# Block 2 of a two-block transformer: where x's norm and transposes stand, and a pool for the merged features

## The chip, the cores and the metric

The kernel runs on one core of a Trainium2 chip. Its time is that of one execution on the device, in microseconds (us). The core's engines are TensorE (PE; its weight loads are shown as PEld), VectorE (DVE), ScalarE (ACT), GpSimd (POOL) and SyncE (SP), whose queue issues the DMAs.

## What is computed

Block 1 (two layers on 256 tokens of x) is not touched. Block 2 works on x and on 256 tokens of a context, ctx, in two layers; only x is returned, so layer 1 doesn't update ctx.

```python
for l in range(2):
    with_ctx = l < 1
    # sh, sc, g: shift, scale, gate of x; csh, csc, cg: of ctx
    u, uc = x * (1 + sc1) + sh1, ctx * (1 + csc1) + csh1
    y, yc = token_mixer(u, uc, ...)   # conv, mLSTM, attention branches; gated merge; @ w_out + b_out
    x = layer_norm(alpha * x + g1 * y, ln1_g, ln1_b)
    x = layer_norm(alpha * x + g2 * sq_relu_mlp(x * (1 + sc2) + sh2, w1, b1, w2, b2), ln2_g, ln2_b)
    if with_ctx:
        ctx = layer_norm(alpha * ctx + cg1 * yc, ln1_g, ln1_b)
        ctx = layer_norm(alpha * ctx + cg2 * sq_relu_mlp(ctx * (1 + csc2) + csh2, ...), ln2_g, ln2_b)
```

The width is 1024, the feed-forward's 4096. All is float32; a product is made of three matmuls on high and low halves.

## The kernel before

**Tokens.** Block 2 holds four tiles of 128 tokens, `self.res[0..3]`: 0 and 1 are ctx, 2 and 3 are x. In transposed tiles (features on partitions) ctx has columns 0 to 255 and x columns 256 to 511. Layer 0 works on all four, layer 1 needs ctx only as a source of keys, values and states, so its later parts work on x's 256 columns alone.

**Products.** `w` loads a weight tile of 512 KB (`wr`, SP's queue), ScalarE makes its high half (`wh`, L323), and VectorE the low half (`wl`, L326); while the counter `self.spare` is positive, GpSimd makes `wl` instead. Four buffers of each rotate. `mm3` (L331 to L333) issues the three matmuls. `tiles` (L350) works several weight tiles over column ranges that are given as `parts`.

**From tokens to u.** `ln` (L955 to L972) makes a token tile's norm: statistics on VectorE, the power -0.5 on GpSimd (L368), the two halves of the row on ScalarE (L970) and VectorE (L972). `make_u` (L933 to L940) takes a stream (two token tiles) in four steps; a step has four transposes on PE into a PSUM tile `tp` (two of them exist), a scale and shift by ScalarE (L938) and VectorE (L940), and the split into high (`uh`, ScalarE, L391) and low (`ul`, VectorE, L392). `uT` takes `uh` and `ul` from a pool that holds one pair of 512 columns.

**The order in a layer.** `layer` runs: make_u of what is left; `residual` (GpSimd, L885 to L902); `mixer2`, which merges three gated branches into `macc` (L1019, L1020) and splits it (L1474 and on) into a pair from `uT`; then w_out (`for n in range(2)`), whose products `tail` (L1562 to L1565) adds to the tokens. For n = 0 one group of matmuls serves all tokens, for n = 1 each token is a group, in the order 3, 2, 1, 0, with its norm behind it. Then a pool `ff` opens, u is made again, and `mlp` runs: `up` and `down` over eight chunks of 512 hidden features. The first chunk's four tiles are worked for x's columns first, then for ctx's. The last `down` of layer 0 has two groups of 48 matmuls, tokens 0 and 1, then 2 and 3. When `mlp` is over the four tokens are normed, and layer 1 starts with make_u of ctx, then of x; its mixer begins with two tiles of `w_in`, for ctx's columns and then for x's.

**What sets the order.** A planner orders each engine's instructions ahead of the run. It goes by the place in the program, an instruction that stands earlier going first, and by its own estimate of when an instruction is ready; one that is estimated to be ready may pass one that isn't. On the chip every engine works its list in order. Pools of tiles are stacked: a pool that opens where another was closed gets its space, and waits for its last reader. `mixer2`'s last pool of gates (`sh`, tiles `sg`) is closed right before the pool `tl` of w_out opens at its place.

## Time and profile before

| | us |
|---|---|
| median of three runs | 2396.82 (2395.77 to 2398.0) |
| the profiled execution | 2396.18 |
| its span, first to last instruction | 2394.4 |
| PE busy | 2310.1 |
| DVE busy | 1747.2 |
| ACT busy | 1195.4 |
| POOL busy | 382.0 |

The profile is that of one execution. A row of its timeline gives the start in us from the span's start, the length, the engine, the line, the operation, what it writes and reads, and in brackets how long the engine stood still before it and what it waited for. Matmuls overlap, so a matmul's length is not its cost; the distance of two starts is. PEclk is the granted clock of TensorE as a share of 2.4 GHz; it is 1.00 or, at the lower level of 1.2 GHz, 0.50, and a window's value is the mean.

### The profile page before, as it was taken

Reading aid. Unit: us, or ns where it says so; the run is one execution under the profiler, and the core shown is the slowest. Engines: PE = TensorE matmul, PEld = TensorE weight load, DVE = VectorE, ACT = ScalarE, POOL = GpSimd, SP = SyncE. Lnnn points to the kernel's source line nnn. Section 1 sums busy time; section 2 is a strip of 40 time slices with the busy share of each in tenths; the row PEclk is TensorE's granted clock in tenths of the full one; section 3 lists DMA queues with packets and bytes.
Section 4 is the critical chain, followed back from the end, with each engine's and each line's share of the span. In section 5 each row is a group of like instructions: output and inputs, shape, how many; then the busy total and the mean of one; then the engine's idle time right before and its main releaser. Section 6 shows DMA issues by size and latency. Waiting matters only on the chain. (4 is left out here: it accounts for less than half of the span.)

```text
span 2394.4 us, 35555 instructions
## 1 busy us (share of the span) xinstructions
PE 2310.1 (96%) x13796; PEld 1965.8 (82%) x13796; DVE 1747.2 (73%) x2632; ACT 1195.4 (50%) x1827; POOL 382.0 (16%) x230
## 2 busy tenths in 40 slices
PE   7999999999999999999999998999998999998997
PEld 6899978888999888788777876777787888897896
DVE  7876778897666589946745559777658996857657
ACT  6766667774465544443443324333334455645553
POOL 4522324550000110000000035000005000003102
PEclk9999999999999999999999999999999999999999
DMA  7544546775555553222214434565433433446553
GB/s 260 180 158 153 161 161 207 248 245 185 185 177 186 188 175 106 75 80 72 87 46 145 136 117 137 181 199 175 127 96 115 150 103 115 133 150 195 188 189 106
DMA packets 120665, 364.64 MB, mean 152 GB/s; under 512 B 28529, under 2 KB 30321, under 8 KB 120497
## 3 DMA queue, kind: packets, MB, share of 16 engines
q1 hardware_dynamic: 120496, 362.38, 47.4%
q8 instruction: 108, 1.77, 0.3%
q14 instruction: 61, 0.49, 0.1%
HBM read 359.05 MB, written 3.28 MB: 151 GB/s over the span
## 5 line engine op out<-in xcount | busy, mean ns | idle before, releaser
L323 ACT CAST wh<-wr 128x1024 fp32r<-128x1024 f32 (+1 forms) x544 | 566.4, 1043 | 791.7 <-PE mm L332 424.0
L326 DVE TENSOR_TENSOR wl<-wr,wh 128x1024 fp32r<-128x1024 f32 x528 | 677.3, 1287 | 325.2 <-ACT wh L323 320.1
L332 PE MATMUL mm<-ul,wh 128*128 128x256 f32 (+1 forms) x2224 | 709.4, 321 | 6.4 <-DVE ul L392 6.4
L333 PE MATMUL mm<-uh,wl 128*128 128x256 f32 (+1 forms) x2224 | 707.9, 320 | 2.6 <-DVE wl L326 2.6
L331 PE MATMUL mm<-uh,wh 128*128 128x256 f32 (+1 forms) x2224 | 704.6, 323 | 4.8 <-ACT uh L424 2.2
L332 PEld LDWEIGHTS mm<-ul,wh 128*128 128x128 f32 x2224 | 421.0, 189 | 45.6 <-DVE ul L392 7.5
L331 PEld LDWEIGHTS mm<-uh,wh 128*128 128x128 f32 x2224 | 415.8, 190 | 47.7 <-issue 7.1
L333 PEld LDWEIGHTS mm<-uh,wl 128*128 128x128 f32 x2224 | 420.2, 189 | 40.6 <-issue 5.2
L332 PE MATMUL mm<-wl,hh 128*128 128x512 f32 x640 | 252.9, 395 | 2.8 <-DVE wl L326 2.8
L331 PE MATMUL mm<-wh,hh 128*128 128x512 f32 x640 | 253.4, 397 | 0.0
L333 PE MATMUL mm<-wh,hl 128*128 128x512 f32 x640 | 253.2, 396 | 0.0
L847 POOL TENSOR_TENSOR macd<-macd,mpr 128x512 f32<-128x512 f32 x108 | 181.6, 1682 | 202.2 <-ACT mpr L846 115.2
L332 PE MATMUL mm<-wl,uh 128*128 128x256 f32 (+1 forms) x672 | 203.5, 304 | 5.8 <-DVE wl L326 5.8
L331 PE MATMUL mm<-wh,uh 128*128 128x256 f32 (+1 forms) x672 | 203.9, 306 | 2.2 <-ACT qk L541 1.5
L843 DVE SCALAR_TENSOR_TENSOR macd<-mr,silu_c,macd 128x512 f32<-128x512 f32 x228 | 189.3, 867 | 22.3 <-POOL macd L847 10.7
L333 PE MATMUL mm<-wh,ul 128*128 128x256 f32 (+1 forms) x672 | 200.8, 301 | 0.1
L331 PEld LDWEIGHTS mm<-wh,hh 128*128 128x128 f32 x640 | 120.8, 189 | 35.1 <-issue 7.5
L332 PEld LDWEIGHTS mm<-wl,hh 128*128 128x128 f32 x640 | 120.8, 189 | 31.7 <-DVE wl L326 3.1
L333 PEld LDWEIGHTS mm<-wh,hl 128*128 128x128 f32 x640 | 120.7, 189 | 28.8 <-issue 0.8
L332 PEld LDWEIGHTS mm<-wl,uh 128*128 128x128 f32 x672 | 127.8, 190 | 14.7 <-DVE wl L326 7.8
L1062 DVE SCALAR_TENSOR_TENSOR cy<-hpad,vecl,cy 128x512 f32<-128x512 f32 (+1 forms) x240 | 138.0, 609 | 0.1
L331 PEld LDWEIGHTS mm<-wh,uh 128*128 128x128 f32 x672 | 127.3, 190 | 12.7 <-ACT qk L541 2.8
(295 smaller groups left out, 3053.6 us busy)
## 6 DMA issues: line engine op xcount, KB each, us to landing
wr<-in_m SPq DMA_DIRECT2D x128, 512.0 KB
wr<-in_w SPq DMA_DIRECT2D x128, 512.0 KB
wr<-in_w_in SPq DMA_DIRECT2D x116, 512.0 KB
mr<-in_w_mod SPq DMA_DIRECT2D x96, 512.0 KB
wr<-in_a_wqkv SPq DMA_DIRECT2D x72, 512.0 KB
wr<-in_b_win SPq DMA_DIRECT2D x24, 512.0 KB
wr<-in_w_out SPq DMA_DIRECT2D x16, 512.0 KB
wr<-in_w_uq SPq DMA_DIRECT2D x16, 384.0 KB
```

The source lines that it names most:

```text
L323: nc.scalar.copy(hi[:, :n], raw[:, :n])
L326: e.tensor_tensor(lo[:, :n], raw[:, :n], hi[:, :n].bitcast(F32), ALU.subtract)
L331: mm(out, lh, rh, start=first, stop=False)
L332: mm(out, lh, rl, start=False, stop=False)
L333: mm(out, ll, rh, start=False, stop=last)
L843: nc.vector.scalar_tensor_tensor(out=a, in0=raw[:, k], scalar=sc, in1=a, op0=ALU.mult, op1=ALU.add)
L847: nc.gpsimd.tensor_tensor(a, a, pr, ALU.add)
L1062: nc.vector.scalar_tensor_tensor(out=ys[ft], in0=src, scalar=wk, in1=ys[ft], op0=ALU.mult, op1=ALU.add)
```

## The change

Four things change in block 2. (1) In layer 0's last `down` the group of tokens 2 and 3 comes first; behind its tails `ready` starts layer 1 (vector load, affine), norms tokens 2 and 3 and makes x's u, and behind the second group it does the same for ctx. The norm and make_u at the start of layer 1 go. (2) Layer 1's first `tiles` has four tiles (two more of the conv branch), x's columns of all four first, then ctx's columns of the first two. (3) The merged features get tiles `mo_h` and `mo_l` in the pool `tl`, split when the mixer is over; u for the feed-forward is taken ahead of w_out, and make_u of x stands right behind token 2's norm, that of ctx behind token 0's. (4) In that pool the gate rows have two buffers, not six.

```diff
@@ -350,8 +350,10 @@
     def tiles(self, aps, uh, ul, c0, c1, parts):
 
         Ws, pts = [], []
-        for k0, k1, a, b in parts:
+        for k0, k1, a, b, *of in parts:
             for i, ap in enumerate(aps):
+                if of and i not in of[0]:
+                    continue
                 if len(Ws) == i:
                     Ws.append(self.w(ap, KT, P))
                     pts.append(self.ps())
@@ -682,7 +684,7 @@
         o, n = self.vat[name]
         return self.vs[:, o:o + n]
 
-    def mlp(self, uh, ul, c0, c1, w1, w2, bias, evac, first):
+    def mlp(self, uh, ul, c0, c1, w1, w2, bias, evac, first, ready=None):
 
         nc, n = self.nc, c1 - c0
 
@@ -713,7 +715,7 @@
         def down(hc, hid):
             groups = [([nn], range(n // P)) for nn in range(2)]
             if hc == 7 and bias is not None:
-                groups = [([0, 1], range(j, j + 2)) for j in range(0, n // P, 2)] if n == 512 else [([0, 1], [j]) for j in range(2)]
+                groups = [([0, 1], [j, j + 1]) for j in (2, 0)] if n == 512 else [([0, 1], [j]) for j in range(2)]
             if hc == 7 and n == 256 and bias is not None:
                 self.spare = TE
             Ws = {}
@@ -728,6 +730,8 @@
                 for nn in nns:
                     for j in js:
                         evac(j, nn, hc, pts[nn, j])
+                if hc == 7 and n == 512:
+                    ready(js)
                 if hc == 7 and nns == [0]:
                     self.halfway()
                 self.tick(MT)
@@ -865,13 +869,13 @@
         self.gdr[l] = self.t(self.dp, [2, 6, D], f"gdr{l}")
 
 
-    def row(self, ap):
-        r = self.t(self.lp, [P, D], "row", bufs=6)
+    def row(self, ap, bufs=6):
+        r = self.t(self.lp, [P, D], "row", bufs=bufs)
         self.nc.sync.dma_start(r, ap.broadcast_to([P, D]))
         return r
 
-    def gate_row(self, l, sub, s):
-        return self.row(self.gdr[l][1 - s:2 - s, sub * 3 + 2, :])
+    def gate_row(self, l, sub, s, bufs=6):
+        return self.row(self.gdr[l][1 - s:2 - s, sub * 3 + 2, :], bufs)
 
     def residual(self, l, sub, toks, prev):
 
@@ -1401,8 +1405,12 @@
                 nc.sync.dma_start(self.tabq, A["c_tab"][:, 0:512])
                 nc.sync.dma_start(tabk, A["c_tab"][:, 512:1536])
                 self.spare = SP[2]
-                tis = [0, 1] + ([T_CONV, T_CONV + 1] if l == 0 else [])
-                p1, p2, *pre = self.tiles([A[f"w_in_{l}"][ti, 0] for ti in tis], uh, ul, 0, 512, ((0, KT, 0, 256), (0, KT, 256, 512)))
+                tis = [0, 1, T_CONV, T_CONV + 1]
+                p1, p2, *pre = self.tiles([A[f"w_in_{l}"][ti, 0] for ti in tis], uh, ul, 0, 512,
+                                           ((0, KT, 0, 256), (0, KT, 256, 512)) if l == 0 else
+                                           ((0, KT, 256, 512), (0, KT, 0, 256, (0, 1))))
+                if l:
+                    pre = [p_[:, 256:512] for p_ in pre]
                 krt = self.t(xg, [P, 512], "krt")
                 h_ = slice(64, 128)
                 for dst, src, ti in ((kr2, p1, 0), (krt, p2, 1)):
@@ -1462,19 +1470,19 @@
             for ft in range(4):
                 self.split(b[0][:, ft, :], b[1][:, ft, :], cy[:, ft, :])
             self.run(self.branch_merge(l, 0, "w_conv", b[0], b[1], acc, uh, ul, sgs))
-        mh, ml = self.uT()
-        for k in range(KT):
-            self.split(mh[:, k, q0:512], ml[:, k, q0:512], acc[:, k, :])
-        return mh, ml
+        return acc
 
     def start(self, l):
 
         self.vl = self.t(self.xp, [P, max(self.A[f"vec{j}"].shape[1] for j in range(2))], "vecl", bufs=2)
         self.nc.sync.dma_start(self.vl[:, 0:self.A[f"vec{l}"].shape[1]], self.A[f"vec{l}"])
         aff = self.affine(l, 0, *((None, None) if l == 0 else (self.vecl(f"prev_g_{l}", 0, KT), self.vecl(f"prev_b_{l}", 0, KT))))
-        self.u = self.uT()
-        yield from self.make_u([0], aff, *self.u)
-        self.aff = aff
+        self.u, self.aff = self.uT(), aff
+
+    def start_ctx(self):
+
+        self.start(0)
+        yield from self.make_u([0], self.aff, *self.u)
         yield
 
     def layer(self, l):
@@ -1484,10 +1492,9 @@
         toks = [0, 1, 2, 3] if l == 0 else [2, 3]
         prev = None if l == 0 else (l - 1) * 6 + 4
         spill = l == 0
-        if l:
-            self.run(self.start(l))
         uh, ul = self.u
-        self.run(self.make_u([1], self.aff, uh, ul))
+        if l == 0:
+            self.run(self.make_u([1], self.aff, uh, ul))
         with tc.tile_pool(name=f"prep{l}", bufs=1) as self.lp:
             self.residual(l, 0, toks, prev)
             if spill:
@@ -1498,14 +1505,19 @@
             self.rc.close()
             self.rp.close()
         with tc.tile_pool(name=f"mix{l}", bufs=1) as self.xq:
-            mh, ml = self.mixer2(l, uh, ul, toks)
+            acc = self.mixer2(l, uh, ul, toks)
             if spill:
                 rp = self.rp.enter_context(tc.tile_pool(name="res1", bufs=1, side="right"))
                 self.res = [self.t(rp, [P, D], f"resb{j}") for j in range(4)]
                 for j in toks:
                     nc.sync.dma_start(self.res[j], xbd[j])
             with tc.tile_pool(name=f"tl{l}", bufs=1) as self.lp:
-                G = {s: self.gate_row(l, 0, s) for s in sorted({j // 2 for j in toks})}
+                mh, ml = (self.t(self.lp, [P, KT, 512 - q0], t, F32R) for t in ("mo_h", "mo_l"))
+                for k in range(KT):
+                    self.split(mh[:, k, :], ml[:, k, :], acc[:, k, :])
+                u = self.uT()
+                aff = self.affine(l, 1, self.vecl(f"ln1_g_{l}", 0, KT), self.vecl(f"ln1_b_{l}", 0, KT))
+                G = {s: self.gate_row(l, 0, s, 2) for s in sorted({j // 2 for j in toks})}
                 for n in range(2):
                     Ws = {}
                     for js in ([toks[::-1]] if n == 0 else [[j] for j in toks[::-1]]):
@@ -1514,17 +1526,17 @@
                             if kc not in Ws:
                                 Ws[kc] = self.w(A[f"w_out_{l}"][n, kc], 2, 512)
                             for j in js:
-                                self.lin_t(pts[j], Ws[kc], 0, 512, mh, ml, j * P, k0=kc * 2, first=kc == 0, last=kc == 3)
+                                self.lin_t(pts[j], Ws[kc], 0, 512, mh, ml, j * P - q0, k0=kc * 2, first=kc == 0, last=kc == 3)
                         for j in js:
                             self.tail(j, n, pts[j], G[j // 2], 0.5)
                             if n == 1:
                                 self.ln([j])
+                                if j % 2 == 0:
+                                    self.run(self.make_u([j // 2], aff, *u))
         with ExitStack() as cx:
             self.xm = cx.enter_context(tc.tile_pool(name=f"ff{l}", bufs=1))
             self.lp = self.xm
-            uh, ul = self.uT()
-            aff = self.affine(l, 1, self.vecl(f"ln1_g_{l}", 0, KT), self.vecl(f"ln1_b_{l}", 0, KT))
-            self.run(self.make_u([1, 0] if l == 0 else [1], aff, uh, ul))
+            uh, ul = u
             with self.behind():
                 G = self.residual(l, 1, toks, l * 6 + 1)
             accs = [self.t(self.xm, [P, D], f"facc{j}") for j in toks]
@@ -1546,13 +1558,20 @@
                 for i in range(2):
                     nc.sync.dma_start(self.last[i], A["rows"][10 + i:11 + i].broadcast_to([P, D]))
             self.spare = SP[1][l]
+
+            def ready(js):
+
+                if l == 0:
+                    if js[0] == 2:
+                        self.drain_bg()
+                        self.start(1)
+                    self.ln(js)
+                    self.run(self.make_u([js[0] // 2], self.aff, *self.u))
             self.mlp(uh, ul, q0, 512, A[f"w1_{l}"], A[f"w2_{l}"], lambda f: self.vecl(f"b1_{l}", f), evac,
-                     ((0, KT, 256, 512), (0, KT, 0, 256)) if l == 0 else ((0, KT, 256, 512),))
+                     ((0, KT, 256, 512), (0, KT, 0, 256)) if l == 0 else ((0, KT, 256, 512),), ready)
             self.drain_bg()
             if l:
                 self.finish()
-        if l == 0:
-            self.ln(toks)
 
     def tail(self, j, n, src, G, f=None):
         e = self.nc.vector
@@ -1621,7 +1640,7 @@
                     self.mixer_b()
                     for j in range(2):
                         self.tap("b1c", self.res[2 + j], j)
-                    self.bg.append(self.start(0))
+                    self.bg.append(self.start_ctx())
                     self.mlp1(1, u2)
                     for j in range(2):
                         self.tap("b1d", self.res[2 + j], j)
```

## Rows read from the trace of the kernel before

**Rows 1.** Engines on the page: busy us, share, instructions.

```profile
PE 2310.1 (96%) x13796; PEld 1965.8 (82%) x13796; DVE 1747.2 (73%) x2632; ACT 1195.4 (50%) x1827; POOL 382.0 (16%) x230
```

**Rows 2.** Waits in stretch A: engine, line, released by; us, times, longest.

```profile
PE tp L933 <- DVE mt L940: 4.9, 1, 4.9
...
PE mm L332 <- DVE ul L392: 2.2, 2, 1.4
```

**Rows 3.** The same view of stretch B.

```profile
PE mm L332 <- DVE ul L392: 4.2, 3, 2.9
PE tp L933 <- DVE mt L940: 4.1, 1, 4.1
```

**Rows 4.** Sums of A, B, dense: busy (count) PE PEld DVE ACT POOL, PEclk.

```profile
1414.81:1451.18 36.37, 29.23 (x226) 28.45 (x224) 27.93 (x28) 17.22 (x27) 32.29 (x14) 0.91 0.41 145
1816.11:1843.71 27.60, 19.27 (x133) 18.38 (x131) 25.05 (x38) 11.10 (x19) 22.23 (x12) 0.88 0.46 155
1846.00:1866.00 20.00, 20.00 (x171) 20.00 (x170) 18.82 (x24) 17.68 (x24) 2.25 (x1) 1.00 0.58 198
```

**Rows 5.** The same sums, around low clock, and one with full clock.

```profile
1418.55:1425.38 6.83, 4.60 (x22) 4.61 (x23) 6.66 (x11) 3.35 (x6) 4.86 (x3) 0.50 0.55 187
1821.32:1824.73 3.41, 3.41 (x16) 3.41 (x17) 3.41 (x11) 2.67 (x5) 1.52 (x3) 0.50 0.90 219
1838.39:1841.80 3.41, 3.41 (x18) 3.41 (x18) 3.17 (x4) 1.49 (x3) 3.41 (x2) 0.50 0.02 5
2000.00:2006.00 6.00, 4.34 (x38) 4.17 (x37) 5.20 (x9) 3.21 (x6) 0.66 (x1) 1.00 0.46 123
```

**Rows 6.** Timeline of PE: start us, us, line, tiles [idle before, releaser].

```profile
1420.78 1.11 PE L933 MATMUL tp<-cst,resb 128*128 128x128 f32 x4 [4.93 <-DVE mt L940]
...
1888.99 0.48 PE L1192 MATMUL mm<-m_q,m_k 128*128 128x256 f32 x1 [3.39 <-DVE m_k L1164]
...
2003.01 0.35 PE L388 MATMUL mm<-cst,l_a 128*128 128x1 f32 x2 [1.66 <-DVE l_a L1273]
...
2189.96 0.48 PE L933 MATMUL tp<-cst,resb 128*128 128x128 f32 x1 [7.29 <-ACT resb L970]
```

**Rows 7.** Timeline of POOL: casts of weights in A and in B.

```profile
1412.01 2.41 POOL L326 TENSOR_TENSOR wl<-wr,wh 128x1024 fp32r<-128x1024 f32 x1 [4.12 <-ACT wh L323]
...
1809.03 2.41 POOL L326 TENSOR_TENSOR wl<-wr,wh 128x1024 fp32r<-128x1024 f32 x1
1811.88 8.27 POOL L326 TENSOR_TENSOR wl<-wr,wh 128x1024 fp32r<-128x1024 f32 x3 [0.44 <-ACT wh L323]
```

**Rows 8.** Timeline of DVE: a norm, second half in A, B.

```profile
1408.06 0.54 DVE L972 TENSOR_SCALAR resb<-resb,bmv,brs 128x512 f32<-128x512 f32 x1
...
1809.92 1.80 DVE L972 TENSOR_SCALAR resb<-resb,bmv,brs 128x512 f32<-128x512 f32 x1
```

**Rows 9.** Lines of DVE in A, B: count, busy us, mean ns.

```profile
L392 DVE TENSOR_TENSOR ul<-mt,uh 128x512 fp32r<-128x512 f32 x8 | 12.6, 1604 | 0.3 <-ACT uh L391 0.2
...
L392 DVE TENSOR_TENSOR ul<-mt,uh 128x512 fp32r<-128x512 f32 x8 | 10.6, 1329 | 0.4 <-ACT uh L391 0.4
```

**Rows 10.** Timeline of DVE: end of the merge, layers 0, 1.

```profile
1368.93 1.46 DVE L392 TENSOR_TENSOR ul<-macc,uh 128x512 fp32r<-128x512 f32 x2
1370.40 0.69 DVE L1019 SCALAR_TENSOR_TENSOR mt<-sg,mm 128x512 f32<-128x512 f32 x1
...
2161.04 0.41 DVE L1019 SCALAR_TENSOR_TENSOR mt<-sg,mm 128x256 f32<-128x256 f32 x1
```

**Rows 11.** Timeline of PE: last branch matmul, first of w_out.

```profile
1369.96 0.40 PE L333 MATMUL mm<-b_h,wl 128*128 128x512 f32 x1
1370.20 0.39 PE L331 MATMUL mm<-wh,uh 128*128 128x512 f32 x1
```

**Rows 12.** Waits of SP's queue at w_out's start, layer 0.

```profile
SPq L870 <- DVE mt L1019: 3.8, 1, 3.8
```

**Rows 13.** Timeline of ACT: a cast of merged features, layer 0.

```profile
1369.05 0.62 ACT L391 CAST uh<-macc 128x512 fp32r<-128x512 f32 x1 [0.86 <-DVE macc L1020]
```

## The prediction, made before the change was built

> **What bounds the kernel now.** I read the page first: TensorE (PE) is busy 96% of the span [rows 1], so only two things can move the end: time in which PE stands still, and time in which it runs at the lower clock. Next came the waits of PE in the two stretches that the change rearranges, then the window sums of these stretches for the granted clock, and last the timelines of DVE and POOL there. I call the stretches A (layer 0, from w_out's last matmul to the end of the feed-forward's first four tiles, 36.37 us), B (from layer 0's last feed-forward matmul to the end of layer 1's first two tiles, 27.60 us) and C (layer 1's w_out to its feed-forward).
>
> In A PE waits 4.9 us at a transpose for the evacuation of the one before it (L940) and 2.2 us at matmuls for the low half of u (L392), 7.1 us in all [rows 2]. In B it is 4.1 + 4.2 = 8.3 us [rows 3]. Nothing else ends PE's idle time there. The reader should see that all waits are on the chain norm, transpose, scale, split of make_u: no weights, no DMA. The mean granted clock is 0.91 in A and 0.88 in B, against 1.00 in a dense stretch [rows 4]. It is the lower level, 1.2 GHz (0.50), for 6.83 us in A and twice 3.41 us in B, after PE had stood for 4.9, 4.1 and 2.9 us [rows 2, 3, 5]; a wait of 1.66 us left the clock at 1.00 [rows 5, 6]. In A the low stretch begins at 1418.55 while PE still stands until 1420.78 [rows 5, 6], so 1425.38 - 1420.78 = 4.6 us are worked at half speed: 2.3 us lost. In B 6.82 us at half speed lose 3.4 us.
>
> So A loses 7.1 + 2.3 = **9.4 us** and B 8.3 + 3.4 = **11.7 us**. A second count agrees: a matmul of 256 columns takes 20.00 / 170 = 0.118 us in the dense stretch [rows 4]; A holds 192 of them (22.6 us) and 32 transposes at some 0.11 us (3.5 us, the spacing of dense ones), so 10.3 of its 36.37 us are not work. At most 21.1 us are to be had, 0.9% of the time.
>
> **Part 1, B.** In layer 0's last down pass x's tokens (2, 3) come first, then ctx's. The group of ctx's tokens is 48 matmuls of 512 columns, each 0.24 us behind the one before [rows 11], so 11 us, and x's norm, 16 transposes and their splits move beneath it. No matmul or transpose is added; 2 x 24 matmuls of the two conv tiles move forward (5.7 us that PE would do just behind, so they only change places). After that PE has x's columns of four tiles, 4 x 24 x 0.118 = 11.3 us, to cover ctx's norm and transposes. Before, the group that ended first had its norm done on DVE at 1811.72 and the group's matmuls lasted to 1816.1, so some 4.4 us remain for four steps of scale and split. Each step occupies DVE for one L940 (some 0.54 us, as the L972 at 1408.06 of the same kind and size [rows 8]) and one L392 (0.73 us [rows 10]), 5.1 us in all, if nobody is in the way.
>
> Somebody is. POOL subtracts the first four weight tiles' low halves from 1809.03 on, 2.4 to 2.8 us each and to 1820.15 [rows 7], and DVE operations are longer whenever POOL works: the second norm pass (L972) took 1.80 us there and 0.54 us at 1408.06, where POOL stood [rows 8]; L392 averaged 1.60 us in A and 1.33 in B [rows 9] against 0.73 a piece at 1368.93, far from any POOL work [rows 10]. The Trainium skill (SBUF — State Buffer, Who interferes with whom) says that a DVE instruction with two SBUF inputs and a GpSimd instruction that reads SBUF exclude each other, the later one blocking fully; the trace agrees in kind, though its means lie below a whole POOL operation. Were the price a whole POOL operation for each of the moved L392, the slower rival below would come out.
>
> With 0.6 to 0.9 us more for each of four L392 (2.4 to 3.5 us), x's u comes 3 to 5 us late for the matmuls behind it. PE works its queue in order, so this shows either as a stall at a transpose inside the down matmuls or at x's first tile, not both. Ctx's part then meets POOL's residual work (L885 to L902), but under 11.3 us of matmuls; I allow 1 us. Left of B's 11.7: **5 us**. Bounds: 1 us (planned well), 11 us (every L392 stalls PE as now); I stay near the middle, as the means [rows 9] are measured in this very contention. Gain in B: **6.7 us**.
>
> What is queued behind the new waits: DVE's tails of ctx's tokens stand behind the splits and free the accumulators which x's third and fourth tile need; these start 5.7 us after the first, which covers that. SP gets the layer's vector load and no other DMA earlier; POOL gets x's rsqrt among its casts in place of ctx's. The conv tiles' inputs come earlier, and layer 1's gate chain has 5.7 us less of matmuls behind it; it ends in a tight spot already, PE's 3.39 us at m_k [rows 6]. Cost between -3 and +3 us; I take none, because m_k depends on the order on DVE and not on the gates.
>
> **Part 2, A.** Make_u of x goes right behind token 2's norm, so its transposes and splits run under w_out's last two groups (24 matmuls of 512 each, 11 us). Here POOL is free until 1412.01 [rows 7], and x's norm is over at 1408.60 [rows 8]: 3.4 us without contention, then some. The u tiles are free since the mixer is over, which is what the own pool is for. I leave 1.5 us for x's part. Ctx's norm still follows the last matmul. In C the same chain, from the last matmul to the first transpose, takes 7.29 us [rows 6], and four steps of make_u some 6 us more, 13.3 in all. The cover is four tiles of x, 11.3 us. So ctx is late by about 2 us: left **3.5 us** of 9.4 (bounds 1 and 8). Gain in A: **5.9 us**.
>
> **Part 3, the pool of the merged features.** This is the price. Before, the splits of macc went into u's tiles while the last branch's matmuls ran, and w_out began without a gap (at 1370.20, 0.24 us behind the branch's last matmul [rows 11], and as closely in layer 1). The new tiles mo_h, mo_l open where the closed pool of the last gates (sg) lay. A tile at that place already shows what this means: the gate row's DMA, first in the same pool, waited 3.8 us in layer 0 for L1019, the last reader of sg [rows 12], and in layer 1 for the same line. So the first split can only start when the last L1019 ends, 1371.09 in layer 0 [rows 10]. Then one cast of 0.62 us [rows 13] and w_out can start at about 1371.8: **1.6 us** of stall, and DVE's low half (0.73 us, behind a 1.2 us weight subtraction or not) adds 0 to 0.9 us. In layer 1 the last L1019 ends at 2161.45 [rows 10], though without the splits in its way it comes about 0.8 us sooner; a cast of half width takes some 0.4 us, so w_out starts at 2161.1 to 2161.9 and not at 2160.2: 0.9 to 1.7 us. Sum 2.5 to 4.2 us. If a stall lets the clock fall (it did not after 1.66 us, it did after 2.9), 1.7 us come on top in one layer: upper bound 6. I take **3.6 us**, a little above the middle. A lower bound below zero has no reason behind it, since the splits were fully hidden before.
>
> **C** is unchanged: layer 1's w_out ends with token 2 and make_u needs both tokens, so the 7.29 us wait for the norm [rows 6] stays; two small affine operations move away, 0 us.
>
> **The sum.** 6.7 + 5.9 - 3.6 = 9.0 us. The profiled execution took 2396.18 us (span 2394.4 and 1.8 around it); 2396.18 - 9.0 = 2387.2. It lies 0.6 us below the median of 2396.82, so the forecast for a median is **2388**.
>
> **The rivals.**
> (a) The waits only move into the matmuls. The planner sets x's transposes by its own estimate of the norm; if DVE is late at every step, PE stands ahead of ready matmuls. With 8 us left in A and 10 in B and 4.5 for the pool: 21.1 - 18 - 4.5, about 1 us slower, 2398, no change to be measured. For it: POOL's casts lie exactly there in B. Against: in A POOL stands for the first 3.4 us. Also here: the planner puts the transposes behind the matmuls after all, so that the change does not do what it says, with 21.1 us lost again and the pool's 3.6: about 2400 if no more cover comes from four tiles, 2394 with it. Chance 0.2.
> (b) Slower. Each moved L392 waits for a whole POOL operation, 2.8 us in B's mean [rows 7], four times at each place, and the clock falls after each: 2 x (11.2 + 2.3) + 5 for the pool = 32 against 21.1, 2396.8 + 11 = 2408. It decides from about 2.0 us per L392 on, where loss and gain are 4.8 us apart; the total lengths of 1.3 to 1.6 us [rows 9] speak against it. Chance 0.07.
> (c) Everything fits: A and B leave 1 us each, the pool 2.5: 21.1 - 4.5 = 16.6 us, 2380. For it: 11 us of matmuls lie over every moved chain. Against: POOL. Chance 0.1.
> The forecast (some 5 to 14 us gained, 2383 to 2392) has 0.63.
>
> **The numbers.** About 0.2% (4.8 us) is what a measurement of this kernel can tell from no change. Faster than 2392.0: the forecast and (c), 0.73. Within 2392.0 to 2401.6: (a), 0.20. Slower: 0.07. The range runs from (c) at 2380 to 2397, which takes in the pool's upper bound together with a left of 7 and 9 us.
>
> **What the changed profile would show.** The waits of PE on L940 and L392 in A and B fall from 15.4 us to some 6; the granted clock over both windows rises above 0.95. New: PE waits at w_out's first matmuls for the casts of mo_h, some 1.6 us in layer 0 and 1 in layer 1, each right behind the last L1019. C's 7.3 us are as before. I am wrong if PE stalls at transposes inside w_out or the last down pass for more than 4 us each, if w_out's stall passes 3 us, or if the wait at m_k grows by what B saves.

## The result, and the profile after

The changed kernel takes 2421.97 us (median; 2421.33 to 2422.76), the kernel before beside it on the same chip 2396.30: a ratio of 1.0104 (95% interval 1.0091 to 1.0116), 25.7 us slower. The prediction said 2388, range 2380 to 2397, with 0.07 for slower. The profiled execution has a span of 2420.97 us for 2394.39.

The page's engines, after (answers to [rows 1]):

```profile
PE 2317.2 (96%) x13787; PEld 1969.5 (81%) x13796; DVE 1753.8 (72%) x2632; ACT 1194.1 (49%) x1827; POOL 381.6 (16%) x230
```

The work is the same; PE is busy 7 us longer and stands some 20 us longer. PE's waits over the whole span, after (what waited, released by; us, times, longest):

```profile
PE tp L855 <- issue: 13.3, 1, 13.3
PE mm L332 <- DVE wl L326: 8.9, 10, 3.1
PE mm L332 <- DVE ul L394: 7.9, 5, 3.5
PE tp L1150 <- DVE g_li L1142: 7.2, 1, 7.2
PE tp L937 <- ACT resb L974: 7.2, 1, 7.2
PE tp L937 <- DVE mt L944: 7.2, 3, 4.6
```

L855 is the matmul of ones behind layer 1's modulation (L851 before), L1150 the transposes of the gate rows (L1146), L937 make_u's transposes (L933), L394 the low halves (L392). Of the three longest single waits, the prediction has the 7.17 us at L937, takes the place of the 7.19 us for safe, and doesn't name that of the 13.34 us at all. PE's timeline, after, at the gaps (start, length, [idle before, releaser]):

```profile
1370.93 0.47 PE L331 MATMUL mm<-wh,mo_h 128*128 128x512 f32 x1 [1.58 <-ACT mo_h L393]
...
1418.84 1.11 PE L937 MATMUL tp<-cst,resb 128*128 128x128 f32 x8 [2.17 <-DVE mt L944]
1423.92 0.39 PE L332 MATMUL mm<-ul,wh 128*128 128x256 f32 x1 [3.49 <-DVE ul L394]
...
1463.14 1.89 PE L855 MATMUL tp<-macd,cst 128*32 128x512 f32 x2 [13.34 <-issue]
...
1831.66 1.97 PE L937 MATMUL tp<-cst,resb 128*128 128x128 f32 x8 [4.61 <-DVE mt L944]
...
1872.83 0.39 PE L331 MATMUL mm<-uh,wh 128*128 128x256 f32 x1 [2.31 <-ACT g_z L1118]
...
1909.10 0.64 PE L1150 MATMUL tp<-cst,g_li 36*128 36x36 f32 x4 [7.19 <-DVE g_li L1142]
...
2183.83 0.47 PE L331 MATMUL mm<-wh,mo_h 128*128 128x512 f32 x1 [1.42 <-ACT mo_h L393]
...
2213.89 1.97 PE L937 MATMUL tp<-cst,resb 128*128 128x128 f32 x8 [7.17 <-ACT resb L974]
```

Window sums, after: A, the low clock around the 13.34 us, the 27.9 us behind layer 0's last FF matmul (B was 27.6), the low clock at the gate rows (columns as in [rows 4]):

```profile
1416.67:1449.80 33.13, 27.47 (x216) 27.02 (x216) 28.71 (x33) 16.50 (x26) 24.56 (x11) 0.95 0.55 208
1451.84:1468.91 17.07, 5.54 (x9) 2.18 (x9) 17.07 (x7) 1.70 (x2) 16.99 (x7) 0.50 0.19 57
1827.06:1855.00 27.94, 20.75 (x150) 20.34 (x150) 22.73 (x38) 10.61 (x16) 18.57 (x9) 0.88 0.44 142
1905.82:1916.06 10.24, 5.37 (x17) 4.15 (x18) 10.18 (x25) 5.65 (x16) 0.15 (x2) 0.50 0.45 148
```

A itself became 3.2 us shorter (33.13 for 36.37). The loss lies behind it. I cut every trace at the same points: w_out's first and last matmul of layer 0; the tenth of the modulation's twelve matmuls of ones, which stands in the dense middle of FF (the expectation of v2 calls it the sixth); FF's last matmul; the first scores (`m_q,m_k`). "Start of FF" is from w_out's last matmul to that tenth, "border" from FF's last matmul to the first scores.

| us | before | after | difference |
|---|---|---|---|
| to w_out's first matmul | 1370.20 | 1370.93 | 0.7 |
| w_out | 44.77 | 45.73 | 1.0 |
| start of FF | 247.95 | 256.18 | 8.2 |
| rest of FF | 153.35 | 154.21 | 0.9 |
| border | 72.72 | 85.36 | 12.6 |
| the rest | 505.40 | 508.56 | 3.2 |

The first row differs by up to 4 us between kernels that are alike up to there (1366.6 to 1370.7 in those without the new pool), so it proves nothing by itself.

### The profile page after: what moved, and what is told of

Its sections match the earlier page's. It is cut to its first block, busy times and chain, and to the rows that moved or that the text cites. A ratio compares the mean times of both kernels' runs of the same rounds, so it can differ in the third digit from the quotient of the medians.

```text
span 2421.0 us, 35549 instructions
## 1 busy us (share of the span) xinstructions
PE 2317.2 (96%) x13787; PEld 1969.5 (81%) x13796; DVE 1753.8 (72%) x2632; ACT 1194.1 (49%) x1827; POOL 381.6 (16%) x230
## 5 line engine op out<-in xcount | busy, mean ns | idle before, releaser
L847 DVE SCALAR_TENSOR_TENSOR macd<-mr,silu_c,macd 128x512 f32<-128x512 f32 x228 | 199.7, 911 | 18.9 <-POOL macd L851 10.7
L851 POOL TENSOR_TENSOR macd<-macd,mpr 128x512 f32<-128x512 f32 x108 | 181.3, 1679 | 202.1 <-ACT mpr L850 115.6
L332 PE MATMUL mm<-wl,uh 128*128 128x256 f32 x576 | 166.0, 289 | 5.9 <-DVE wl L326 5.9
L331 PE MATMUL mm<-wh,uh 128*128 128x256 f32 x576 | 166.5, 291 | 2.2 <-ACT qk L543 1.4
L333 PE MATMUL mm<-wh,ul 128*128 128x256 f32 x576 | 163.6, 285 | 0.1
L333 PEld LDWEIGHTS mm<-wh,hl 128*128 128x128 f32 x640 | 121.0, 189 | 28.7 <-issue 0.8
L332 PEld LDWEIGHTS mm<-wl,uh 128*128 128x128 f32 x576 | 109.5, 190 | 10.6 <-DVE wl L326 7.8
L331 PEld LDWEIGHTS mm<-wh,uh 128*128 128x128 f32 x576 | 109.2, 190 | 8.5 <-issue 2.7
```

What stands on the lines that cost most here:

```text
L331: mm(out, lh, rh, start=first, stop=False)
L332: mm(out, lh, rl, start=False, stop=False)
L333: mm(out, ll, rh, start=False, stop=last)
L847: nc.vector.scalar_tensor_tensor(out=a, in0=raw[:, k], scalar=sc, in1=a, op0=ALU.mult, op1=ALU.add)
L851: nc.gpsimd.tensor_tensor(a, a, pr, ALU.add)
```

## The experiments

All are edits of the kernel before or of the changed one; ratios are to the kernel before, run beside them, with a 95% interval. That kernel's median lay between 2394.6 and 2396.5 us in these rounds, so differences in us are taken within a round. Stretches are from one profile of each run.

| run | us | ratio | start of FF | border |
|---|---|---|---|---|
| before, 16 KB set aside (e1_pad) | 2409.1 | 1.0058 (1.0043 to 1.0073) | 260.6 | 74.4 |
| changed, buffers apart (e2_apart) | 2416.3 | 1.0094 (1.0077 to 1.0111) | 251.9 | 85.7 |
| part of w_out alone (e3_a_only) | 2404.4 | 1.0042 (1.0027 to 1.0056) | 251.8 | 72.8 |
| pool alone (p3_pool_only) | 2399.7 | 1.0020 (1.0011 to 1.0029) | 246.5 | 72.5 |
| border alone (e4_b_only) | 2403.8 | 1.0039 (1.0024 to 1.0054) | 248.4 | 82.1 |
| before, residuals out (q0) | 2379.2 | 0.9929 (0.9912 to 0.9946) | 237.8 | 69.8 |
| e2_apart, residuals out (q1) | 2390.0 | 0.9976 (0.9966 to 0.9985) | 235.7 | 76.8 |
| before, residuals on DVE (v0) | 2393.5 | 0.9993 (0.9984 to 1.0003) | 240.0 | 80.4 |
| e2_apart, residuals on DVE (v1) | 2400.8 | 1.0019 (1.0009 to 1.0028) | 242.5 | 80.6 |
| before, FF's residual on DVE (v2) | 2387.9 | 0.9968 (0.9956 to 0.9981) | 239.7 | 73.0 |
| e3_a_only, FF's residual on DVE (v3) | 2394.9 | 1.0000 (0.9992 to 1.0009) | 242.1 | 72.8 |
| border alone, two tiles (b1) | 2404.6 | 1.0040 (1.0027 to 1.0054) | 248.5 | 82.2 |
| border alone, ctx first (b3) | 2408.6 | 1.0054 (1.0037 to 1.0071) | 248.3 | 82.0 |
| before, taps out (t0) | 2386.6 | 0.9963 (0.9948 to 0.9977) | 248.3 | 68.2 |
| border alone, taps out (t1) | 2398.3 | 1.0010 (1.0000 to 1.0019) | 248.7 | 75.9 |
| border alone, casts on DVE (b5) | 2407.4 | 1.0040 (1.0025 to 1.0055) | 248.5 | 85.0 |
| b5 without residual (b6) | 2396.6 | 0.9999 (0.9990 to 1.0008) | 248.4 | 74.9 |
| before in the same condition (c6) | 2393.0 | 0.9986 (0.9976 to 0.9995) | 247.8 | 71.4 |

**The modulation's buffers.** In the kernel before, layer 1's modulation starts long before FF: its first weights are loaded at 1304.26, under the mixer. In the changed kernel they come at 1421.18, behind w_out's last tail. SP's timeline (before; after):

```profile
1304.26 0.80 SPq L836 DMA_DIRECT2D mr<-in_w_mod  x2
```

```profile
1421.18 0.80 SPq L840 DMA_DIRECT2D mr<-in_w_mod  x2
```

Its sums on DVE then fall into POOL's residual, as DVE's timeline of after shows:

```profile
1428.85 3.40 DVE L847 SCALAR_TENSOR_TENSOR macd<-mr,silu_c,macd 128x512 f32<-128x512 f32 x5
1443.59 19.45 DVE L847 SCALAR_TENSOR_TENSOR macd<-mr,silu_c,macd 128x512 f32<-128x512 f32 x7
```

Seven of them take 19.45 us, 2.78 apiece, where five took 3.40, and the matmul of ones behind FF's first four tiles waits for the last, which ends at 1463.04: the 13.34 us (the profile names no releaser there). The reason is an address: w_out's pool, longer by the merged features, now ends at 200896, and the modulation's sums begin at 196544 (the addresses are those of the compiled kernel, not of the profile). Two runs test this from both sides.

```diff
 with tc.tile_pool(name=f"tl{l}", bufs=1) as self.lp:      # e1_pad, on the kernel before
+    if l == 0:
+        self.t(self.lp, [P, 4096], "pad")
```

> The kernel before, with 16 KB of SBUF set aside and never used in layer 0's pool of the output projection, so that this pool ends at 200896 as in the changed kernel; nothing else differs. Theory (space): the buffers in which layer 1's modulation adds up its weights (196544 to 210880) now overlap that pool, their first loads wait for its last tail, and the matmul of ones at L851, which stands right behind FF's first four tiles in PE's order, waits as in the changed kernel (13.3 us, and 17.1 us at half clock behind it); less what the kernel before pays a little later at the same line (4.8 us): 2408 to 2418. Rival (the moved norm and transposes, or the new order of tiles, made the changed kernel slow): none of them is in this kernel, 2395 to 2398.

```diff
-t = self.t(self.lp, [P, 512], "tl", bufs=2)               # e2_apart, on the changed kernel
+t = self.t(self.lp, [P, 512], "tl", bufs=2) if f is None else self.t(self.xp, [P, 512], "mt", bufs=2)
 ...
+self.t(self.xm, [P, 64], "pad")                           # ahead of the pool mod1
```

> The changed kernel, whose output projection takes the tails' temporary from the tile pool that the split's temporaries use, so that its pool ends at 196800, and FF's pool is 256 bytes longer, so that the modulation's buffers begin at 196800: no overlap, nothing else differs. Theory (space): the 13.3 us stall at the matmul of ones goes and with it most of the 17.1 us at half clock behind it, 15 to 20 us of the 25: 2402 to 2407. Rival (the moved work itself is what costs): 2419 to 2423.

The empty tile alone makes the kernel before 14.5 us slower: the loads come at 1419.13 there, and nothing of the change is in it. So the overlap is a cause by itself. The time came as expected, but not the place: at L851 PE waits 2.1 and 1.6 us, and more of the loss lies at u's low halves and in low clock behind them (at 0.50 from 1445.9 to 1459.6 and from 1463.0 to 1473.2). PE's timeline, e1_pad:

```profile
1448.19 0.58 PE L332 MATMUL mm<-ul,wh 128*128 128x256 f32 x1 [5.56 <-DVE ul L392]
...
1462.12 1.07 PE L851 MATMUL tp<-macd,cst 128*32 128x512 f32 x2 [2.12 <-issue]
```

Taking the overlap out of the changed kernel gives back only 5.7 us (4.0, if each is counted from the kernel before of its own round), and another 22 us are left: the theory missed in e2_apart. In e2_apart PE waits 5.39 and 7.25 us a little later at the same place. My expectation also counted the low clock wrongly: of the 17.07 us at 0.50 PE stands until 1463.14, and only some 5.3 are worked, 2.7 lost.

"Nothing else differs" in that expectation is not true either. `mt` has two buffers, and make_u's scaled tiles use them too. In the program x's four steps stand ahead of ctx's tails, so with the tails' temporary in `mt` ctx's two last tails must wait for x's casts: they start 9.1 us behind the end of w_out's last matmul. In the changed kernel itself the tail of token 1 runs 6.4 us ahead of that matmul's end, as in the kernel before (DVE's timeline, after):

```profile
1410.25 0.69 DVE L1583 SCALAR_TENSOR_TENSOR tl<-mm,row 128x512 f32<-128x512 f32 x1 [0.86 <-PE mm L333]
...
1419.16 0.67 DVE L1583 SCALAR_TENSOR_TENSOR tl<-mm,row 128x512 f32<-128x512 f32 x1
```

So e2_apart shows what is left without the overlap, and with this wait put in. The runs made from it (e3_a_only, p3_pool_only, q1, v1, v3) share the buffers.

**Each part alone.** e3_a_only undoes the border's parts in e2_apart:

```diff
-groups = [([0, 1], [j, j + 1]) for j in (2, 0)]           # n == 512
+groups = [([0, 1], range(j, j + 2)) for j in range(0, n // P, 2)]
-ready(js)                                                 # norm and make_u back at the end of layer 0 and the start of layer 1
-tis = [0, 1, T_CONV, T_CONV + 1]
+tis = [0, 1] + ([T_CONV, T_CONV + 1] if l == 0 else [])
```

p3_pool_only is e3_a_only with make_u back behind w_out, e4_b_only the changed kernel with w_out's part undone, and with it the overlap:

```diff
-if j % 2 == 0:                                            # p3_pool_only and e4_b_only
-    self.run(self.make_u([j // 2], aff, *u))
 ...
+self.run(self.make_u([1, 0] if l == 0 else [1], aff, uh, ul))
-mh, ml = (self.t(self.lp, [P, KT, 512 - q0], t, F32R) for t in ("mo_h", "mo_l"))   # e4_b_only
+mh, ml = self.uT()
```

> The kernel of the run before this one with the parts at the layers' border taken back (old order of the last down projection, ctx's norm and transposes first, two tiles of gates in layer 1): only the merged features' own pool and the transposes under the output projection are left, and the modulation's buffers apart. Theory (space): the stretch between the output projection and FF gains some 3 to 6 us, the pool costs 3.0 us (the stalls of 1.6 and 1.4 us that the changed kernel shows): 2392 to 2397. Rival (transposes under matmuls cost more than the stretch behind them saves): 2400 to 2410.

> The kernel before with the merged features' own pool alone: their casts are written there, the modulation's buffers stand apart, and all norm and transposes are where they were. The prediction put this at plus 3.6 us (bounds 2.5 to 6): 2397 to 2401. What the other runs show for it by their stretches: a stall of 1.6 us and a projection longer by 1.0 in layer 0, a stall of 1.4 in layer 1: plus 3 to 4.5, the same. Rival (the pool also moves the loads of FF's rows and so POOL's residual, with the price that the part with the transposes showed, near 10 us): 2402 to 2406.

> The changed kernel with the output projection and FF's first tiles as before (features in the old place, transposes behind the projection): only the parts at the layers' border are left. Theory 2 (the gate chain has lost its cover): from the border to the first scores the changed kernel took 85.5 us where the kernel before took 72.9: plus 8 to 13, 2404 to 2409. The prediction's own step: minus 6.7, 2390. Rival (all of the loss is the modulation's, the border costs nothing): 2394 to 2398.

The pool costs 4.6 us (2.6 to 6.9), as its step said; the shared buffers change the order of no tail there, but FF's rows load 0.8 us behind w_out's last matmul and not 5.4, and the start of FF is 1.4 us shorter than in the kernel before, so the pool by itself may cost a little more. The transposes under w_out, the other half of e3_a_only, cost 5.2 more (9.8 less 4.6; the intervals leave some 4 us either way), together with the late tails of the shared buffers: no run separates the two. The border's parts cost 9.2 where 6.7 were to be gained, and e4_b_only has the old tails. 9.8 and 9.2 make 19.0 of e2_apart's 21.7.

**Where A's gain goes in e3_a_only.** There the stretch does what was forecast: PE waits 0.62, 1.39 and 0.86 us where it waited 7.1 [rows 2], the mean clock is 0.95 (1417.35 to 1453.50), and the four tiles end 31.0 us behind w_out for 36.4, 5.4 us gained. PE's timeline, e3_a_only, then shows what follows:

```profile
1419.05 0.74 PE L331 MATMUL mm<-uh,wh 128*128 128x256 f32 x4 [0.62 <-ACT uh L393]
1421.18 0.39 PE L332 MATMUL mm<-ul,wh 128*128 128x256 f32 x1 [1.39 <-DVE ul L394]
1435.88 1.11 PE L935 MATMUL tp<-cst,resb 128*128 128x128 f32 x8 [0.86 <-DVE mt L942]
...
1477.61 0.80 PE L332 MATMUL mm<-wl,hh 128*128 128x512 f32 x1 [5.47 <-DVE wl L326]
1485.66 1.91 PE L853 MATMUL tp<-macd,cst 128*32 128x512 f32 x2 [7.25 <-DVE macd L845]
```

The kernel before has at these places:

```profile
1479.54 1.51 PE L851 MATMUL tp<-macd,cst 128*32 128x512 f32 x2 [4.81 <-DVE macd L843]
```

The chain is in the timelines. DVE, e3_a_only: x's casts (L394) meet POOL's weight casts, two of them take 4.87 us, and ctx's tails (L1583, L1584) stand behind them, for want of a buffer.

```profile
1419.03 4.87 DVE L394 TENSOR_TENSOR ul<-mt,uh 128x512 fp32r<-128x512 f32 x2 [1.31 <-ACT uh L393]
...
1425.10 1.42 DVE L394 TENSOR_TENSOR ul<-mt,uh 128x512 fp32r<-128x512 f32 x2
1426.44 1.28 DVE L1583 SCALAR_TENSOR_TENSOR mt<-mm,row 128x512 f32<-128x512 f32 x2
```

FF's rows wait on SP's queue for the last reader of w_out's pool (waits of SP's queue, e3_a_only), so POOL starts the residual at 1434.43 and not at 1427.49, and ends it 7.0 us later; counted from the end of w_out's last matmul it starts at 17.1 us for 12.5 and ends at 58.5 for 53.9 (POOL's timeline, first and last row, e3_a_only; then before):

```profile
SPq L872 <- DVE mt L1583: 4.0, 1, 4.0
```

```profile
1434.43 2.78 POOL L887 TENSOR_SCALAR row<-row 128x1024 f32<-128x1024 f32 x1 [2.66 <-issue]
...
1469.87 6.00 POOL L904 TENSOR_TENSOR resb<-resb,row 128x1024 f32<-128x1024 f32 x2
```

```profile
1427.49 2.78 POOL L885 TENSOR_SCALAR row<-row 128x1024 f32<-128x1024 f32 x1 [3.39 <-DMA row<-in_rows]
...
1463.33 5.57 POOL L902 TENSOR_TENSOR resb<-resb,row 128x1024 f32<-128x1024 f32 x2
```

In the changed kernel it starts 15.8 us behind that matmul and ends at 54.7. There FF's rows stand behind the late loads of the modulation on SP's queue and not behind late tails, and in e1_pad, where only the overlap is new, it starts at 17.6 (POOL's timeline, after):

```profile
1432.43 2.78 POOL L889 TENSOR_SCALAR row<-row 128x1024 f32<-128x1024 f32 x1 [6.16 <-DMA row<-in_rows]
```

In e3_a_only the later residual falls on FF's first casts and the modulation's sums, which PE needs next. The modulation's sums on DVE from 1450 to 1500 (count, busy us, mean ns) in the kernel before, in e3_a_only and in q0, where the residual is left out:

```profile
L843 DVE SCALAR_TENSOR_TENSOR macd<-mr,silu_c,macd 128x512 f32<-128x512 f32 x28 | 25.7, 973 | 2.0 <-DMA mr<-in_w_mod 2.0
```

```profile
L845 DVE SCALAR_TENSOR_TENSOR macd<-mr,silu_c,macd 128x512 f32<-128x512 f32 x24 | 29.4, 1276 | 0.1
```

```profile
L843 DVE SCALAR_TENSOR_TENSOR macd<-mr,silu_c,macd 128x512 f32<-128x512 f32 x33 | 22.7, 741 | 1.2 <-DMA mr<-in_w_mod 1.2
```

The next runs take the suspect away (q0, q1) or give its work to DVE (v0 to v3):

```diff
-e = nc.gpsimd                                             # v0, v1; v2 and v3 for (0, 1) alone
+e = nc.vector if (l, sub) in ((0, 1), (1, 0)) else nc.gpsimd
 ...
+if (l, sub) in ((0, 1), (1, 0)):                          # q0, q1
+    return {s: self.gate_row(l, sub, s) for s in sorted({j // 2 for j in toks})}
```

> The kernel before; left out is the whole work of two residuals, that in front of layer 0's FF and that in front of layer 1's mixer (16 and 8 POOL operations of 128x1024, some 41 and 22 us of POOL from 1427 and 1827 on, and the loads of their rows; the gate rows stay). While POOL does them, DVE's operations with two inputs take 2.4 to 3.4 us where they take 0.7 to 1.2 elsewhere. Theory (POOL's residuals hold DVE up, and DVE holds PE up at both places): the waits of 0.8, 1.4, 4.8 us (layer 0) and 0.5, 2.9, 0.8 us (layer 1) go, with some low clock: 8 to 15 us less, 2380 to 2388. Rival (the waits come from the length of the chain, whatever POOL does): under 3 us less, 2392 to 2397.

> The changed kernel with the modulation's buffers apart (2416.3 us), with the same two residuals left out as in the run before this one. Theory (the moved norm and transposes push these residuals some 7 us later, onto FF's first casts and the modulation's sums, and that takes back more than the move gains): without them the moves gain what was forecast or part of it, so 0 to 6 us less than the kernel before without them, after 3 us for the features' pool: 2376 to 2388. Rival (DVE's queue or the gate chain is late whatever POOL does): it stays 10 us or more above the kernel before without them, 2392 to 2405.

> The kernel before, its two residuals' operations issued on DVE in place of POOL; nothing is left out. On DVE a 128x1024 operation with two inputs takes 1.2 us, so 16 and 8 of them put 20 and 10 us on DVE, which was busy 47.1 of the 50 us from 1450 to 1500. Theory (contention with POOL costs DVE more than that: in the changed kernel with A alone six sums of the modulation took 2.88 us for 0.74, and casts 2.8 to 3.4 for 1.2): 2 to 8 us less, 2387 to 2393. Rival (DVE has no room for it): 5 to 20 us more, 2400 to 2415.

> The changed kernel with the modulation's buffers apart (2416.3 us), its two residuals' operations issued on DVE in place of POOL; nothing is left out. Theory (the loss is the residuals' contention, moved onto FF's start and ctx's transposes): 10 to 20 us less, 2397 to 2406. Rival (gate chain and DVE's queue are late anyway, and the residuals only add to DVE): 2415 to 2435.

> The kernel before with one thing changed: the residual in front of layer 0's FF is computed on DVE and not on POOL (16 operations of 128x1024); the one at the border of the layers stays on POOL. In the run that put both on DVE, the stretch from the last matmul of the output projection to the sixth sum of the modulation took 240.0 us for 248.0, and the border 80.4 for 72.7. Theory (contention in the first, DVE queue ahead of the gate chain in the second): only the gain is left, some 8 us: 2385 to 2390. Rival (the two runs differ by chance or the one pays for the other): 2392 to 2396.

> The kernel with the output projection's part alone (features' pool, transposes under the projection; 2404.4 us), its residual in front of FF computed on DVE and not on POOL. Theory (POOL's residual, pushed 7 us later, is what takes back the gain of the moved transposes): against the run before this one the moved transposes now gain about 2 us behind the projection, as they did where the residual was left out (235.7 for 237.8), and the pool costs 3 to 4: 2386 to 2392, 0 to 3 above the run before. Rival (the moved work costs by itself): 6 to 10 above it, 2393 to 2399.

POOL's residual costs the start of FF 10.2 us in the kernel before (247.95 less 237.8) and 16.2 with the moved transposes (251.9 less 235.7): without it the moved parts gain 2.1 us there, with it they lose 3.9. So 6.0 us are shown to hang on POOL's residual; that they come from its shift is read from the timelines, and the shift is that of e2_apart's tails. As a whole q1 missed: it stays 10.8 us above q0, as its rival had it, most of it at the border (7.0). q0 is 15.8 us faster, as expected or a little more. v0 comes out even: its start of FF is 8 us shorter and its border 7.7 longer, where DVE has the gate chain to do. v1 gained 15 us on e2_apart, as expected. v2 is the fastest that leaves nothing out, 7.2 us faster than the kernel before (4.6 to 10.5). v3 missed: it stays 7.0 us above v2, 4.6 of them the pool's. With the residual on DVE, PE waits 3.96 us at ctx's transposes for L942, as it waited 4.93 at x's in v2: there the wait only moved, and ctx's tails are late there too.

**The border.** In the changed kernel PE waits at L1150 for the gate rows. ACT reads the two gate sums, one per tile, when all columns of u are through; the later read, in the kernel before and in after (ACT's timeline):

```profile
1857.62 0.68 ACT L1113 ACTIVATE g_li<-mm,vecl 36x512 f32<-36x512 f32 x1
```

```profile
1876.82 0.67 ACT L1117 ACTIVATE g_li<-mm,vecl 36x512 f32<-36x512 f32 x1
```

Counted from FF's last matmul (1816.27 and 1827.06) that is 41.4 and 49.8 us. These are the moments of the chain in each run:

| us behind FF's last matmul | last cast of u | second sum read | first scores |
|---|---|---|---|
| before | 27.4 | 41.4 | 72.7 |
| border alone | 37.5 | 49.8 | 82.1 |
| two tiles (b1) | 37.5 | 49.9 | 82.2 |
| ctx first (b3) | 35.6 | 50.6 | 82.0 |
| before, taps out (t0) | 27.7 | 41.7 | 68.2 |
| border alone, taps out (t1) | 38.2 | 50.1 | 75.9 |
| before, no POOL work (c6) | 20.6 | 28.7 | 71.4 |
| border alone, no POOL work (b6) | 23.3 | 31.8 | 74.9 |

My first theory was the four tiles, the second the order of the streams.

```diff
-tis = [0, 1, T_CONV, T_CONV + 1]                          # b1, b3
+tis = [0, 1] + ([T_CONV, T_CONV + 1] if l == 0 else [])
-groups = [([0, 1], [j, j + 1]) for j in (2, 0)]           # b3 alone
+groups = [([0, 1], [j, j + 1]) for j in (0, 2)]
```

> The kernel with the border's parts alone (2403.8 us), but in layer 1 the mixer begins with two tiles, as before the change, and not with four: x's columns of the two gate tiles, then ctx's, and the two tiles of the convolution where they were before. Theory (the border is set by the gate chain, which begins with the last column of the two gate tiles and takes some 31 us from the first read of their sums to the transposes of g_z at any of the kernels; with four tiles x's columns of the convolution stand ahead of ctx's transposes, and the last column of ctx was ready 37.5 us behind the last FF matmul, where the kernel before had all at 27.4): the chain starts some 5 us earlier, and from the last FF matmul to the first scores it takes 75 to 79 us for 82.1: 2397 to 2401. Rival (PE needs the two tiles as cover under ctx's transposes, as the prediction had it): PE waits there instead, 2404 to 2409.

> The kernel with the border's parts alone (2403.8 us), but with the streams in the old order: ctx's tokens are finished first in the last down projection and ctx's norm and transposes stand under x's last matmuls, x's come behind, and the mixer begins with two tiles, ctx's columns first. Theory (the border is set by the gate chain, which waits for the last cast of features: 27.4 us behind the last FF matmul in the kernel before, 37.5 in both kernels with x first; what is first under the matmuls is worth less than what is last behind them): the last cast comes at 25 to 30 again, and from the last FF matmul to the first scores it takes 70 to 75 us for 82.1: 2392 to 2397. Rival (norm and transposes under the last matmuls make the loss, whichever stream it is): 80 to 84, 2402 to 2407.

Both fell. With two tiles PE's rows are the same to 0.2 us, for the planner puts the convolution's tiles in the same place anyway; with ctx first it is x that comes late. What stays in both is that one pair's scales and casts stand on DVE ahead of the other pair's tails and norm: DVE's half of the second pair's norm ends 12.7 us behind FF's last matmul and not 9.0, and all four casts of that pair then meet POOL's residual (three did in the kernel before). The same is seen in e4_b_only (DVE's timeline):

```profile
1835.19 2.64 DVE L394 TENSOR_TENSOR ul<-mt,uh 128x512 fp32r<-128x512 f32 x1 [0.23 <-ACT uh L393]
1841.09 2.87 DVE L394 TENSOR_TENSOR ul<-mt,uh 128x512 fp32r<-128x512 f32 x1
...
1848.44 4.40 DVE L394 TENSOR_TENSOR ul<-mt,uh 128x512 fp32r<-128x512 f32 x2 [0.23 <-ACT uh L393]
```

The next runs shorten the chain behind the sums, and take POOL away.

```diff
-for k in range(1, 31):                                    # t0, t1
+for k in range(1, 31 if l == 0 else 1):
-self.spare = SP[2]                                        # b5, b6, c6; b6 and c6 also leave out residual (1, 0) as in q0
+self.spare = SP[2] if l == 0 else 0
```

> The kernel before; left out are the 120 taps of layer 1's convolution (its first term stays), 0.48 us each on DVE, many of which stand between the steps of the gate chain. Theory (the chain, some 31 us long with them, just keeps up with PE here, so shortening it gains little): the border from the last FF matmul to the first scores takes 68 to 72 us for 72.7, the rest of the gain lies behind it: 2380 to 2392. Rival (the chain is not on the path): 72.7 as before.

> The kernel with the border's parts alone (2403.8 us), with the same 120 taps left out as in the run before this one. Theory (the gate chain ends last and starts some 10 us later than before): without the taps in it the border falls by 5 to 10 us, to 72 to 77 for 82.1, and the distance to the run before this one at the border from 9.4 to 3 to 7 us. Rival (the distance comes from PE's own waits in front of the chain): it stays at 9 to 10.

> The kernel with the border's parts alone (2403.8 us), with the four weight casts that POOL makes under the last down projection (2.4 us each) given to DVE (1.2 each); nothing is left out. In all kernels so far the border follows the moment at which the second sum of the gates is read: 31 to 32 us later come the first scores (before 41.3 and 72.7, border's parts 49.8 and 82.1, ctx first 50.6 and 82.0, two tiles 49.9 and 82.2). Theory (while POOL casts, tails and casts on DVE wait for a whole POOL operation, so the norm of the second pair of tokens, which now has the first pair's casts ahead of it, comes 3.5 us later, and all behind it): the wait of 4.6 us behind the last matmul falls under 2, the second sum comes 4 to 7 us earlier, the border 75 to 78: 2397 to 2400. Rival (the casts on DVE cost what POOL's cost): 81 to 84, 2403 to 2407.

> The kernel of the run before this one; left out is also the work of the residual in front of layer 1's mixer (8 POOL operations), so POOL does nothing but a few small operations at the border. Theory (POOL's work is all that makes the border's parts a loss): the border falls to that of the next run or below it, 62 to 68. Rival (the second pair's norm, transposes and casts come later because the first pair's are ahead of them on DVE and PE, with or without POOL): it stays 5 to 8 us above that of the next run, 72 to 76.

> The kernel before, with the four weight casts under the last down projection on DVE and without the work of the residual in front of layer 1's mixer: the partner of the run before this one. Theory and rival alike: the border at 66 to 70 for 72.7, 2388 to 2393; the distance to the run before this one decides.

Without taps the border gets shorter in both kernels (4.5 and 6.2 us), so DVE's work in front of the first scores, the gate chain among it, is on the path in both. But the distance only falls from 9.4 to 7.7, not to the theory's 3 to 7, and PE then hardly waits for the gate rows, 0.2 us in t1 (waits of PE from FF's last matmul to the first scores, t0, then t1):

```profile
PE mm L332 <- DVE ul L392: 4.5, 3, 2.9
PE tp L933 <- DVE mt L940: 4.1, 1, 4.1
```

```profile
PE tp L937 <- DVE mt L944: 5.2, 2, 4.6
PE mm L332 <- DVE ul L394: 4.4, 3, 2.0
PE mm L331 <- ACT g_z L1118: 2.3, 1, 2.3
...
PE tp L1150 <- DVE g_li L1142: 0.2, 1, 0.2
```

All of them add up to 8.6 us in t0 and 13.8 in t1, where the mean granted clock is 0.91 for 0.95. So PE's own waits ahead of the gates are by themselves enough for most of the distance. With the taps in, these waits are 8.3 us before and 14.4 with the border alone, where PE waits another 2.9 us for the gate rows.

b5 missed as well: POOL's casts given to DVE make the border 85.0, not 75 to 78, though the wait behind the last matmul falls from 4.6 to 3.0; the residual still meets the last casts. Without any POOL work the distance is 3.5 us (74.9 and 71.4; the whole runs 3.6), below the rival's 5 to 8 and above the theory's 0. So POOL's work makes about 5.9 of the border's 9.4 us. (In both, the scores come 43 us behind the second sum and not 31 to 32, so there the sums are not what the border follows.) That the other 3.5 come from the order of DVE's own work is argued from the times above, not shown.

## Why the prediction was wrong, point by point

- **Part 3, right in what it counts.** Stalls of 1.58 and 1.42 us at w_out's first matmuls, no low clock; alone 4.6 us for 3.6, inside 2.5 to 6.
- **C, right.** 7.17 us for 7.29.
- **Part 2, half right in its stretch and wrong in its sum.** "Gain in A: 5.9 us": A gained 3.2 in the changed kernel, and 5.4 with w_out's part alone and the shared buffers. The step that failed is that the sum ended at A's last matmul, and what the moved work does to DVE, SP's queue and POOL behind it was not counted. In the changed kernel the overlap's 13.34 us stand right there and hide it. In e3_a_only the start of FF is 3.8 us longer although A is 5.4 shorter. How much the moved transposes themselves cost or gain stays open: the plus 5.2 us hold the late tails too. For a small gain speaks that the start of FF is 4.4 us shorter in the changed kernel than in e1_pad, which has the overlap alone; w_out is 1.0 longer, and 1.4 the pool's run shows as well.
- **The price of meeting POOL.** I took 0.6 to 0.9 us more for each cast, from means [rows 9]. A mean over casts that meet POOL and casts that don't is no price of either. Where they met, DVE went at POOL's pace: seven sums of the modulation took 2.78 us apiece beside POOL operations of 2.8, and x's casts 4.87 us for two beside casts of 2.4 to 2.8. The Trainium skill (SBUF — State Buffer, Who interferes with whom) says that the later one is blocked fully; these rows agree with it, and I set the rule aside for the mean. Rival (b) had this price, but took its loss at the casts themselves; most of the loss came behind them.
- **Part 1, wrong.** "Gain in B: 6.7 us" came out as plus 9.2 alone. Two steps failed. "But under 11.3 us of matmuls; I allow 1 us" for ctx's part, with 5 us left of B's waits and low clock, is the first: with the border alone PE's waits up to the second gate sum grew from 8.3 to 14.4 us. "Cost between -3 and +3 us; I take none, because m_k depends on the order on DVE and not on the gates" is the second: the gate chain starts with u's last cast, which came at 37.5 us for 27.4, and its second sum was read at 49.8 us for 41.4. Without taps the first alone left 7.7 us of the distance. The 4.1 us behind FF's last matmul [rows 3] did not go either: it is now 4.61, for L944 waits on DVE behind tails that meet POOL's casts. The waits on the scale and the low halves in A and B fell from 15.4 to 11.5 us, not to 6, and the granted clock there is 0.95 and 0.88. Of the three signs named, one came true in a neighbouring place: m_k has 0.3 us left, but the gate rows ahead of it now wait 7.19.
- **Not in the prediction: the pool's end.** Part 3 asked who used the pool's space before and not who uses what lies behind its new end. It costs 14.5 us alone; taking it out of the changed kernel gives back 4.0 to 5.7, in a run that puts the late tails in as well, so what the overlap is worth among the other parts stays open.

The sum of what ran alone: 14.5 (overlap) + 9.2 (border) + 4.6 (pool) = 28.3, against 25.7 to 27.4 measured (the changed kernel against the kernel before of its own round and of the next). The rest, some 1 to 3 us less, is left for the transposes under w_out and for what the parts do to each other, for example 3.3 us more at the border than in e4_b_only; no run parts these. The forecast of a gain failed on the first two, whatever the transposes are worth.

## What to carry to other kernels

When a pool grows, look at what is allocated behind its new end and who was loaded there early. When work is moved ahead on an engine, write down what now stands behind it on that engine, what those instructions release, and follow that down to PE; the sum ends where the order is the old one again, not where the stretch ends. Look at the wait of a chain that just keeps up, as the 3.39 us at m_k: time that PE saves ahead of it may be worth nothing. And an edit that takes one suspect away can put a wait of its own in: look in its trace whether the rest stands where it stood, above all when it lets two uses share buffers.

## What the runs showed of the hardware that I had not expected

The residual is cheaper on the busier engine: on POOL, 14 operations (not the 16 of my expectations) cost the start of FF 10.2 us, on DVE (v2, 239.7 for 237.8 without them) 1.9, although DVE was busy 47 of 50 us there in the kernel before (a sum of the modulation took 973 ns in the mean, and 741 without POOL's work). Low clock cost only where PE worked: of 17.07 us at 0.50 in the changed kernel some 2.7 were lost, in e1_pad some 9 of the 23.9 us at 0.50 named above, of which PE worked 17.8.
